# First block's output product in seven products of quarters, with the per-layer input transposed earlier and the new rows later

## The chip, the cores and the metric

The kernel runs on one core of a Trainium2 chip. The metric is the device time of one execution in microseconds (us), the median of three runs. Below, PE is TensorE (matmul), DVE is VectorE, ACT is ScalarE, POOL is GpSimd, and SP is SyncE, which here only issues transfers.

## What is computed

Two transformer blocks in a row, on 512 tokens of width 1024, in float32. The change touches the output product of the first block, the product of the per-layer input `p` that follows it, and the new rows of `x`:

```python
def first_block(x, p, w_in, b_forget, w_branch_a, w_branch_b, w_merge, w_out,
              g_pre, g_post, w_ple, w_ple_gate, g_ple):
        h = rmsnorm(x, g_pre[i])
        proj = h @ w_in[i]
...
        y_a = (att_a * jax.nn.silu(gate_a)) @ w_branch_a[i]
...
        y_b = (att_b * jax.nn.silu(gate_b)) @ w_branch_b[i]
        m_a, m_b = jnp.split(jax.nn.sigmoid(h @ w_merge[i]), 2, axis=-1)
        out = (m_a * y_a + m_b * y_b) @ w_out[i]      # 512x1024 @ 1024x1024
        x = x + rmsnorm(out, g_post[i])
        e = p[i] @ w_ple[i]                           # 512x256 @ 256x1024
        gate = jax.nn.sigmoid(x @ w_ple_gate[i])
        x = x + rmsnorm(gate * e, g_ple[i])
```

`att_b` is a forgetting attention (FOX below), `att_a` an attention over the 128 keys that an index selects (DSA below).

## The kernel before

Every float32 operand of a product is split into two parts of a shorter float format, high and low, and one product is three matmuls into the same accumulator: high by high, high by low, low by high. A matmul takes 128 rows of the contraction and 512 columns.

**Weights.** All weights are one list of groups (`stream`), in the order of use; a group of a product 512 columns wide is 256 x 512 floats (512 KB). A group is loaded from DRAM by SP into `raw` (line 308; two buffers), ACT writes its high part `wh` (line 333), DVE its low part `wl` (line 334); `wh` and `wl` have four buffers each. When a product has used up group i, `used(i)` has the groups up to three further converted and up to five further loaded. The output product has groups 54 to 61, the attentions' products, gates and branch products those before.

**The output product.** `ev_ya` makes the input of it, `m = m_a y_a + m_b y_b`, chunk by chunk (eight chunks of 128 rows by 512 tokens) and splits each into `mh` (ACT) and `ml` (DVE). `out0` and `out1` are its two halves of 512 columns: four blocks of 128 tokens by eight chunks by three matmuls each, 192 matmuls in all. `ev_out` multiplies by the gain (`ob`), takes the sum of squares on ACT, and in the second half adds to the rows `xr`; `to_T` then transposes the new rows on PE, eight transposes of a block of 128 tokens, and splits them (`x2h`, `x2l`) for the gate product `pg0`, `pg1`. Between stand `e0` and `e1`, the product of `p`, whose transposes (`pst` to `pT`) are made at the start of `out0`.

**Order.** A scheduler (the Tile framework's order of program text plus a planner) sets the order on each engine: an attention head's steps (scores S, softmax on DVE, ACT and POOL, transposes T of the probabilities, values AV) are mixed with matmuls of the products; each engine then goes through its own queue strictly in order. Transposes take turns in two PSUM banks: the next but one can only be written once the splits on ACT and DVE have read the first. In a softmax step POOL does `rr` (line 612) and the scaling of P by it (line 613).

**Sums of weights.** The last product of the kernel (down, line 1404 and on) is already made of seven products of quarters; its weight sums are built in DRAM: `plan_sums` hangs a transfer on a group's conversion. A first copy of a quarter goes by SP, without a wait. The sum is a transfer on POOL's queue that adds in DRAM; ahead of it POOL does a small copy (`poke`, line 248) that waits for that group's `wh`.

Of the kernel before, what the change touches and what calls it, by code (L numbers as in the profile page):

```python
# [11 lines left out]
F32 = mybir.dt.float32  # L12
FR = mybir.dt.float32r
# [15 lines left out]
def two_blocks_kernel(  # L29
# [11 lines left out]
    def unit(name, tag, shape=None, dt=FR):  # L41
        return pool.tile(shape or [128, 8, 512], dt, name=name, tag=tag)
# [35 lines left out]
    AHEAD = 2  # L78
    LATE = {"mla": 3, "pg1": 16, "q2": 8, "o21": 10}
    FOX = (2.0, 2, 2, 1.0)  # L80
# [28 lines left out]
    class Turned:  # L109
# [5 lines left out]
        def split(self, hi, lo, raw):  # L115
# [100 lines left out]

    def down(name):
        if name[0] == "S":  # L220
            return down_sums[name]
        f = DFF // 2 * (name[2] == "2")
        return w_down_2[f:f + DFF // 2, 512 * (name[1] == "2"):512 * (name[1] == "2") + 512]

    down_sums = {f"S{i}": tc.dram_tile([DFF // 2, 512], F32, name=f"down{i}") for i in range(1, 5)}
    DOWN = ("A11", "S4", "A12", "S1", "S2", "S3", "A22")
    specs_tail = {f"dn{name}": ([(down(name), 0, 512, 0)], 11) for name in DOWN}
    behind, poke = {}, pool.tile([128, 1], F32, name="poke", tag="poke")

    def plan_sums():  # L230

        copies = [("S1", "A21"), ("S2", "A11"), ("S4", "A12"), ("S3", "A11")]
        adds = [("S1", "A22"), ("S2", "S1"), ("S4", "S2"), ("S3", "A21")]
        for some, engine, at, step in ((copies, nc.sync, 14, 2), (adds, nc.gpsimd, first_of["seven"], 4)):
            for dst, src in some:
                for r in range(0, DFF // 2, 352):
                    behind[at] = (engine, down_sums[dst][r:r + 352, :], down(src)[r:r + 352, :])
                    at += step

# [739 lines left out]

    mh, ml = unit("mh", "U3"), unit("ml", "U6")  # L980
# [13 lines left out]

    ob = unit("ob", "U2", [128, NB, 1024], F32)
# [4 lines left out]
    x2h, x2l = unit("x2h", "U0"), unit("x2l", "U1")  # L1000

    pst = unit("pst", "U4", [128, NB, 256], F32)
    nc.sync.dma_start(pst, p.rearrange("(b p) d -> p b d", p=128))
    pT = [pool.tile([128, 2, 512], FR, name="pT", tag=f"V{i}") for i in range(2)]
    for tb in range(NB):
        to_T(pst[:, tb, :], 2, pT[0], pT[1], tb)
    gb = g_bcast(g_post)

    def ev_out(nh):
        def f(tb, ps):  # L1010
            nc.vector.tensor_mul(ob[:, tb, 512 * nh:512 * nh + 512], ps, gb[:, 512 * nh:512 * nh + 512])
            sum_sq(ps, ssq[:, tb, nh:nh + 1])
            if nh == 1:
                nc.vector.scalar_tensor_tensor(xr[:, tb, :], ob[:, tb, :], rstd2(ssq[:, tb, :], D), xr[:, tb, :],
                                               op0=OP.mult, op1=OP.add)
                to_T(xr[:, tb, :], 8, x2h, x2l, tb)
        return f
# [5 lines left out]
    eb = unit("eb", "U4", [128, NB, 1024], F32)  # L1023

# [4 lines left out]

    for nh in range(2):  # L1030
        run(product(f"e{nh}", lambda kc: (pT[0][:, kc, :], pT[1][:, kc, :]), ev_e(nh), True))

    gs = unit("gs", "U2", [128, 4, 1024], F32)
    for i, g in enumerate((g_ple, mix_norm_g_2)):
# [511 lines left out]
    def dn_banks(kinds):  # L1546
        return [{"mm": mm_bank, "S": s_bank, "AV": av_bank,
                 "T": lambda: t_bank("E").rearrange("p a b -> p (a b)")}[k]() for k in kinds]

# [23 lines left out]

    DN_ACT = {"A11": "B11", "S4": "B22", "A12": "B21", "S1": "T1", "S2": "T2", "S3": "T3", "A22": "T4"}
    DN_BANK = {"A11": ("S", "S"), "S4": ("T", "T"), "S1": ("mm", "AV"), "S3": ("T", "T"), "A22": ("S", "S")}

    def dn_product(n, name):
# [8 lines left out]
        for i, (kc, b) in enumerate(seq):  # L1586
            if n < 6 and i in (2, 8, 14):
                with tc.issue_after(mark[0]), tc.issue_after(mark_hi[0]):
                    fs_make(DN_ACT[DOWN[n + 1]], i // 6)
# [5 lines left out]
            ah, al = [t[:, kc % 4, blk(b)] for t in fs[DN_ACT[name], kc // 4]]  # L1595
# [65 lines left out]
```

## Time and profile before

| what | value |
|---|---|
| median of 3 runs | 1199.44 us (1199.09 to 1199.97) |
| the profiled execution's own time | 1198.17 us |
| span in that execution, first to last instruction | 1196.4 us |
| PE busy | 1166.9 us (98%), 6634 matmuls and transposes |
| DVE busy | 845.0 us (71%) |
| ACT busy | 637.9 us (53%) |
| POOL busy | 292.3 us (24%) |
| granted TensorE clock, mean over the span | 0.995 of full |

Times in the rows are microseconds from the start of the span. An engine's idle time is only worth something where the engine is the one that the others wait for; here PE has almost none.

### The profile page before, as it was taken

To read this page: it belongs to the slowest core of one execution; us is meant where nothing else is said; L and a number is where in the kernel's file an instruction comes from. 1 tells how busy PE (TensorE), PEld (TensorE's weight loads), DVE (VectorE), ACT (ScalarE), POOL (GpSimd) and SP (SyncE) were. 2 spreads that over 40 slices of the span, in tenths; PEclk is the share of its full clock that TensorE was granted. 3 is DMA by queue.
4 is the path that set the end of the run, shared out by engine and by line. 5 is a ranking of instruction groups with operands and counts; after the bars stand their busy time and mean duration, and the time that the engine had idled before them with its cause. 6 is when DMAs were issued, how large, how long until landed. Compare 5 with 4: busy or idle time off the path is not lost.

```text
span 1196.4 us, 18475 instructions
## 1 busy us (share of the span) xinstructions
PE 1166.9 (98%) x6634; PEld 1009.8 (84%) x6634; DVE 845.0 (71%) x1569; ACT 637.9 (53%) x1260; POOL 292.3 (24%) x500
## 2 busy tenths in 40 slices
PE   7999999999999999999999999999999999999997
PEld 5898888888888888879888878888899999998885
DVE  5578767796565753776445478874698887877895
ACT  4466356535663444544466567752555455556564
POOL 2011065403341020211333435410022212200124
PEclk9999999999999999999999999999999999999999
DMA  5423613443223523324222222155369798857553
GB/s 195 102 92 119 191 48 119 126 137 102 95 71 106 181 85 109 127 90 128 57 71 72 72 60 79 60 158 193 124 127 185 147 190 151 141 132 268 170 184 114
DMA packets 117403, 148.89 MB, mean 124 GB/s; under 512 B 15552, under 2 KB 70080, under 8 KB 117312
## 3 DMA queue, kind: packets, MB, share of 16 engines
q1 hardware_dynamic: 94528, 136.18, 36.2%
q0 software_dynamic: 22784, 11.54, 8.2%
q8 instruction: 52, 0.85, 0.3%
q14 instruction: 39, 0.32, 0.1%
HBM read 141.40 MB, written 29.36 MB: 143 GB/s over the span
## 4 chain that ended last, share of the span: by engine, by line
PE 84%; DVE 4%; issue 4%; ACT 3%; POOL 2%; DMA 2%; SPq 0%; POOLq 0%; ACTq 0%; DVEq 0%
PE mm L422 49%; PE mm L1404 7%; PE E L1404 5%; PE R L1404 5%; PE S L1597 4%; PE AV L666 3%; PE E L1597 3%; PE T L651 2%; PE mm L1597 2%; DVE wl L334 1%; ACT wh L333 1%; DMA raw<-in_w_in_dram 1%; PE T L553 1%; PE S L885 1%; PE S L884 1%
## 5 line engine op out<-in xcount | busy, mean ns | idle before, releaser
L334 DVE TENSOR_TENSOR wl<-raw,wh 128x512 fp32r<-128x512 f32 (+4 forms) x219 | 203.2, 945 | 89.3 <-ACT wh L333 88.4
L333 ACT CAST wh<-raw 128x512 fp32r<-128x512 f32 (+4 forms) x219 | 173.7, 815 | 162.2 <-PE mm L422 65.7
L612 POOL TENSOR_TENSOR rr<-rs,mone 128x1 f32<-128x1 f32 x128 | 75.5, 590 | 166.5 <-ACT P L606 106.0
L522 DVE TENSOR_TENSOR pl<-T,ph 128x128 fp32r<-128x128 f32 (+3 forms) x152 | 61.9, 412 | 60.9 <-ACT ph L521 60.2
L422 PE MATMUL mm<-hh,wh 128*128 128x512 f32 x256 | 103.5, 405 | 0.0
L422 PE MATMUL mm<-hl,wh 128*128 128x512 f32 x256 | 101.4, 396 | 0.0
L422 PE MATMUL mm<-hh,wl 128*128 128x512 f32 x256 | 100.5, 395 | 0.0
L606 ACT ACTIVATE P<-P,nm 128x128 f32<-128x128 f32 (+2 forms) x96 | 51.5, 537 | 51.4 <-DVE nm L599 47.4
L521 ACT CAST ph<-T 128x128 fp32r<-128x128 f32 (+3 forms) x152 | 54.7, 362 | 43.5 <-PE T L651 32.1
L613 POOL TENSOR_SCALAR P<-P,rr 128x256 f32<-128x256 f32 (+3 forms) x128 | 73.4, 573 | 12.0
L333 ACT CAST wh<-qsum 128x1024 fp32r<-128x1024 f32 (+1 forms) x44 | 42.8, 974 | 53.9 <-PE R L1404 16.3
L1404 PE MATMUL R<-acts,wh 128*128 128x256 f32 x320 | 57.8, 281 | 0.0
L1404 PE MATMUL mm<-acts,wh 128*128 128x256 f32 x320 | 57.6, 280 | 0.0
L651 PE MATMUL T<-ident,P 128*128 128x128 f32 x296 | 54.3, 277 | 3.3 <-ACT km L1184 2.4
L422 PEld LDWEIGHTS mm<-hh,wl 128*128 128x128 f32 x256 | 48.0, 188 | 11.2
L1404 PE MATMUL E<-acts,wh 128*128 128x256 f32 x320 | 57.1, 280 | 0.0
L334 DVE TENSOR_TENSOR wl<-qsum,wh 128x1024 fp32r<-128x1024 f32 (+1 forms) x44 | 49.3, 1122 | 11.0 <-ACT wh L333 11.0
L422 PEld LDWEIGHTS mm<-hh,wh 128*128 128x128 f32 x256 | 48.2, 188 | 8.5
L422 PEld LDWEIGHTS mm<-hl,wh 128*128 128x128 f32 x256 | 48.2, 188 | 7.8
L422 PE MATMUL mm<-h2h,wh 128*128 128x512 f32 x128 | 53.6, 419 | 0.0
L422 PE MATMUL mm<-h2h,wl 128*128 128x512 f32 x128 | 50.6, 395 | 0.0
L422 PE MATMUL mm<-h2l,wh 128*128 128x512 f32 x128 | 50.1, 392 | 0.0
(431 smaller groups left out, 3458.8 us busy)
## 6 DMA issues: line engine op xcount, KB each, us to landing
raw<-in_w_in_dram SPq DMA_DIRECT2D x50, 512.0 KB, 3.7
down<-in_w_down_dram SPq DMA_DIRECT2D x16, 704.0 KB, 6.0
quart<-in_w_up_dram SPq DMA_DIRECT2D x20, 512.0 KB, 6.4
raw<-down SPq DMA_DIRECT2D x20, 512.0 KB, 3.9
raw<-in_w_merge_dram SPq DMA_DIRECT2D x16, 512.0 KB, 4.1
raw<-in_w_out_dram SPq DMA_DIRECT2D x16, 512.0 KB, 3.9
quart<-in_w_gate_dram SPq DMA_DIRECT2D x16, 512.0 KB, 5.2
raw<-in_w_down_dram SPq DMA_DIRECT2D x15, 512.0 KB, 4.3
```

Of the source, the lines that this page charges most:

```text
L333: mark_hi[0] = nc.scalar.copy(hi[:, js], raw[:, js]).ins
L334: mark[0] = nc.vector.tensor_sub(lo[:, js], raw[:, js], hi[:, js].bitcast(F32)).ins
L422: nc.tensor.matmul(o, x_, m, start=kc == 0 and k == 0 and n0 == 0, stop=last and k == 2)
L521: nc.scalar.copy(hi, src)
L522: nc.vector.tensor_sub(lo, src, hi.bitcast(F32))
L606: nc.scalar.activation(P[:, :n], P[:, :n], AF.Exp, bias=bias, scale=-1.0, accum_out=rs)
L612: nc.gpsimd.tensor_tensor(rr, rs, mone, op=OP.pow)
L613: nc.gpsimd.tensor_scalar(P[:, :n], P[:, :n], rr, 1.0, op0=OP.mult, op1=OP.mult)
L651: nc.tensor.transpose(T[:, i, :], P[:, blk(i)], ident)
L666: nc.tensor.matmul(self.av[:, q0:q0 + pc.stop - pc.start], self.v(kb), m, start=pi == 0 and i == 0, stop=pi == len(plan) - 1 and i == 1)
L1404: nc.tensor.matmul(R[:, c, :], w[:, kc, cs], m[:, kc, :], start=first and c + kc + k == 0, stop=kc == 3 and k == 2, skip_group_check=True)
L1597: nc.tensor.matmul(acc[b], a, w[:, j], start=first and kc == 0 and k == 0, stop=kc == 10 and k == 2, skip_group_check=True)
```

## The change

The output product is done as seven products on quarters (Winograd's form of Strassen's): the tokens in two halves, the contraction in two halves, the columns in two halves. Each of the seven products is 256 tokens by 512 rows by 512 columns, that is 2 blocks of tokens x 4 chunks x 3 = 24 matmuls. The weights are the quarters A11, A12, A22 and four sums S1 to S4 of quarters, 14 groups in the place of 8; the sums are built in DRAM, by four copies of 1 MB on SP (after the conversions 14, 16, 18, 20) and four adding transfers of 1 MB on POOL (after the conversions 31, 33, 35, 37, with `poke` ahead of each). The sixteen copies for the last product follow from conversion 22 on. The inputs B11, B21, B22 are quarters of `m`, and T1 to T4 their sums: four additions on DVE, and four splits on ACT and DVE. After a product, copies, additions and subtractions in PSUM and SBUF put the four quarters of the result together (`out_end`). The order of `out`, `e0`, `e1` on PE is now that of the text (`ordered()`). The transposes of `pst` move to the start of DSA, and those of the new rows come 16 products later (`LATE`).

```diff
-    LATE = {"mla": 3, "pg1": 16, "q2": 8, "o21": 10}
+    LATE = {"mla": 3, "pg1": 16, "q2": 8, "o21": 10, "out": 16}
...
+    OUT = ("A11", "S4", "A12", "S2", "S1", "S3", "A22")
...
-        "out0": ([(w_out, 0, 512, 0)], 8),
-        "out1": ([(w_out, 512, 512, 0)], 8),
+        **quarters("out", w_out, OUT),
...
+        put(copies, nc.sync, "out", w_out, 512, [14, 16, 18, 20])
+        put([adds[i] for i in (0, 3, 1, 2)], nc.gpsimd, "out", w_out, 512, [31, 33, 35, 37])
+        put(copies, nc.sync, "dn", w_down_2, 352, list(range(22, 54, 2)))
+        put(adds, nc.gpsimd, "dn", w_down_2, 352, list(range(first_of["seven"], first_of["seven"] + 64, 4)))
...
-            elif n >= 0 and n % 5 == 2:
+            elif n >= 0 and n % 5 == 2 or 0 <= m < 14 and m % 3 == 2:
                 raw = pool.tile([128, 1024], F32, name="raw", tag="idx")
...
+    pst = q4("pst", [128, NB, 256])
+    nc.sync.dma_start(pst, p.rearrange("(b p) d -> p b d", p=128))
+    pT = [pool.tile([128, 2, 512], FR, name="pT", tag=f"V{i}") for i in range(2)]
+    for tb in range(NB):
+        to_T(pst[:, tb, :], 2, pT[0], pT[1], tb)
...
-            nc.vector.tensor_add(t, t, acc[:, i, :])
-            split(mh[:, i, :], ml[:, i, :], t, 0.5)
+            m = ta[:, i, :]
+            nc.vector.tensor_add(m, t, acc[:, i, :])
+            if g == 0:
+                split(mp["B11"][0][:, c, :], mp["B11"][1][:, c, :], m[:, 256:], 0.5)
+            else:
+                split(m21[:, 0, c, :], m21[:, 1, c, :], m, 0.5)
...
-                to_T(xr[:, tb, :], 8, x2h, x2l, tb)
+            late.append([LATE["out"], lambda: to_T(xr[:, tb, :], 8, *x2, tb)])
...
+                for k, (a, w) in enumerate(((ah, wh), (ah, wl), (al, wh))):
+                    nc.tensor.matmul(R[into][b], a, w[:, j], start=into == name and kc == 0 and k == 0,
+                                     stop=kc == 3 and k == 2, skip_group_check=True)
+                if i % 4 == 3:
+                    used(f0 + g)
...
+        T = {"T1": ("B11", "B11", OP.subtract, "B12"), "T3": ("B12", "B12", OP.subtract, "B22"),
+             "T2": ("B22", "B11", OP.add, "B22"), "T4": ("B21", "B21", OP.subtract, "B22")}
...
+        some = {(0, 4): lambda: (m_add("T1"), m_add("T3")), (1, 0): lambda: m_add("T2"),
+                (1, 4): lambda: m_part("T2", mp, 0.5), (2, 0): lambda: m_part("T1", mp, 0.5),
+                (2, 4): lambda: m_part("T3", mp, 0.5), (3, 0): lambda: m_add("T4"),
+                (3, 4): lambda: m_part("T4", mp, 0.5)}.get((n, i))
...
+            elif name == "S1":
+                c12 = p2("c12")
+                nc.vector.tensor_sub(c12, R["S4"][b], kept[b])
+                nc.vector.tensor_sub(m_sub[b], m_sub[b], R["S4"][b])
+                ev_out(0, b, c12)
...
-    run(product("out0", pair_act(mh, ml), ev_out(0), True))
-    run(product("out1", pair_act(mh, ml), ev_out(1), True, "tail"))
+    with ordered():
+        for _ in itertools.chain(
+                seven_tok("out", OUT, {"A11": ("AV", "mm"), "S4": ("S", "S"), "U": ("mm", "mm"), "A22": ("AV", "mm")},
+                          mp, out_work, out_end),
+                *[product(f"e{nh}", lambda kc: (pT[0][:, kc, :], pT[1][:, kc, :]), ev_e(nh), True)
+                  for nh in range(2)]):
+            pass
```

DVE, at the end of the branch product `ya1` and the start of the output product. In the rows, `ya<-ta,mm` takes a chunk of y_a from PSUM, the next addition makes it a chunk of m, and `ml` (before) is the low part of the chunk. Before:

```order
L986 SCALAR_TENSOR_TENSOR ya<-ta,mm 128x512 x2
L525 SCALAR_TENSOR_TENSOR ml<-ya,mh 128x512
L987 TENSOR_TENSOR ya<-ya,acc 128x512
L334 TENSOR_TENSOR wl<-raw,wh 128x1024
L987 TENSOR_TENSOR ya<-ya,acc 128x512 x2
L525 SCALAR_TENSOR_TENSOR ml<-ya,mh 128x512 x3
L522 TENSOR_TENSOR pT<-T,pT 128x2x128 x2
```

In the change, from the conversion that stands ahead of the same rows; `m_4116` is `m21`, and the addition at L1085 makes T1 first, then T3:

```order
L347 TENSOR_TENSOR wl<-raw,wh 128x1024
L1013 TENSOR_TENSOR ta<-ya,acc 128x512
L538 SCALAR_TENSOR_TENSOR m_4116<-ta,m_4116 128x512
L1011 SCALAR_TENSOR_TENSOR ya<-ta,mm 128x512 x2
L347 TENSOR_TENSOR wl<-raw,wh 128x1024
L538 SCALAR_TENSOR_TENSOR m_4116<-ta,m_4116 128x512
L1013 TENSOR_TENSOR ta<-ya,acc 128x512 x2
L347 TENSOR_TENSOR wl<-raw,wh 128x1024
L1085 TENSOR_TENSOR ta<-ta 128x4x256
L347 TENSOR_TENSOR wl<-raw,wh 128x1024
L538 SCALAR_TENSOR_TENSOR m_4116<-ta,m_4116 128x512 x2
L1085 TENSOR_TENSOR ta<-ta 128x4x256
```

The low parts of the last two chunks of m now stand behind three conversions and the addition T1; before, behind one conversion.

PE, at the start of DSA, from the third scores (384 keys) of the first head to the first transposed probabilities (`T<-ident,P`); `mm` are matmuls of a product mixed in. Before:

```order
L884 MATMUL S<-kik,qa 128x384
L885 MATMUL S<-kik,qa 128x384
L422 MATMUL mm<-hh,wh 128x512
L422 MATMUL mm<-hl,wh 128x512
L422 MATMUL mm<-hh,wl 128x512
L651 MATMUL T<-ident,P 128x128
```

In the change:

```order
L897 MATMUL S<-kik,qa 128x384
L898 MATMUL S<-kik,qa 128x384
L435 MATMUL mm<-hh,wh 128x512
L435 MATMUL mm<-hl,wh 128x512
L435 MATMUL mm<-hh,wl 128x512
L566 MATMUL T<-ident,pst 128x128 x4
L664 MATMUL T<-ident,P 128x128
```

Four of the eight transposes of `pst`, two to a bank, now stand right ahead of the first `T<-ident,P`; the other four stand, two and two, ahead of the scores of 128 and of 256 keys.

DVE beside it, from the softmax of the first scores (128 keys, `causal`) in the change; `MAX` and `MATCH_REPLACE` are the selection of the keys, `pT` the low parts of the transposed `pst`:

```order
L612 ISA P,nm<-S,causal 128x128
L347 TENSOR_TENSOR wl<-raw,wh 128x1024
L926 MAX m_2792<-mk 128x8
L889 SCALAR_TENSOR_TENSOR aa<-th,mm 128x512
L535 TENSOR_TENSOR pT<-T,pT 128x2x128
L612 ISA P,nm<-S,mk 128x256
L535 TENSOR_TENSOR pT<-T,pT 128x2x128
L927 MATCH_REPLACE mk<-m_2792,mk 128x512
L612 ISA P,nm<-S,mk 128x384
L926 MAX m_2827<-mk 128x8
L535 TENSOR_TENSOR pT<-T,pT 128x2x128 x2
```

Before, no `pT` stands here, and there is one `MAX` and one `MATCH_REPLACE` fewer between the softmax of 128 keys and the end of the selection, since that pair stood ahead of it.

POOL, at the end of FOX, in the change; `outS_81` is S1 in DRAM:

```order
L261 COPY poke<-wh 128x1
L262 DMA outS_81<-in_w_out_dram 512x4x128
L625 TENSOR_TENSOR rr<-rs,mone 128x1
L626 TENSOR_SCALAR P<-P,rr 128x256
L617 TENSOR_SCALAR bias<-nm,ctok 128x1
L625 TENSOR_TENSOR rr<-rs,mone 128x1
L626 TENSOR_SCALAR P<-P,rr 128x384
L617 TENSOR_SCALAR bias<-nm,ctok 128x1
L625 TENSOR_TENSOR rr<-rs,mone 128x1
L626 TENSOR_SCALAR P<-P,rr 128x512
```

Before, the same rows stand there without the first two. The other three pairs of `poke` and transfer (S3, then S2 from S1, then S4 from S2) stand behind the last of these rows, ahead of DSA's first `rr`.

## Rows read from the trace of the kernel before

**Rows 1.** Waits of PE over the whole run: us in total, times, longest.

```profile
PE T L553 <- DVE xn L744: 8.0, 1, 8.0
PE T L553 <- DVE xn L561: 2.7, 1, 2.7
```

**Rows 2.** Busy us by engine (PE, PEld, DVE, ACT, POOL), PEclk, DMA share, GB/s.

```profile
222.00:265.00 43.00, 43.00 (x211) 35.63 (x210) 40.09 (x99) 19.71 (x37) 6.14 (x10) 1.00 0.54 170
...
397.00:412.00 15.00, 15.00 (x71) 12.17 (x70) 11.32 (x17) 6.23 (x10) 0.00 (x0) 1.00 0.83 277
412.00:445.00 33.00, 33.00 (x147) 26.73 (x146) 14.47 (x17) 11.84 (x23) 6.49 (x10) 1.00 0.25 81
445.00:470.00 25.00, 25.00 (x121) 20.49 (x120) 10.80 (x14) 10.20 (x18) 0.93 (x2) 1.00 0.38 126
```

**Rows 3.** Chain that ended last, around the output product: start, us, what.

```profile
411.44 31.25 PE mm L422 x134
```

**Rows 4.** Timeline of DVE at the end of ya1: start, busy us.

```profile
391.60 0.68 DVE L987 TENSOR_TENSOR ya<-ya,acc 128x512 f32<-128x512 f32 x1
392.20 0.68 DVE L525 SCALAR_TENSOR_TENSOR ml<-ya,mh 128x512 fp32r<-128x512 f32 x1
...
397.01 1.21 DVE L334 TENSOR_TENSOR wl<-raw,wh 128x1024 fp32r<-128x1024 f32 x1
398.15 1.27 DVE L986 SCALAR_TENSOR_TENSOR ya<-ta,mm 128x512 f32<-128x512 f32 x2
...
402.89 1.88 DVE L525 SCALAR_TENSOR_TENSOR ml<-ya,mh 128x512 fp32r<-128x512 f32 x3
```

**Rows 5.** Timeline of ACT there.

```profile
395.27 1.06 ACT L333 CAST wh<-raw 128x1024 fp32r<-128x1024 f32 x1 [1.12 <-PE mm L422]
```

**Rows 6.** Groups of DVE by shape, whole run: busy us, mean ns.

```profile
L525 DVE SCALAR_TENSOR_TENSOR fs<-fa,fs 128x1024 fp32r<-128x1024 f32 x14 | 16.9, 1216 | 0.8 <-ACT fs L524 0.8
...
L1503 DVE TENSOR_TENSOR fa<-fa 128x1024 f32<-128x1024 f32 x8 | 10.8, 1352 | 0.0
```

**Rows 7.** Groups of DVE by shape, 375 to 470 us.

```profile
L522 DVE TENSOR_TENSOR pT<-T,pT 128x256 fp32r<-128x256 f32 x4 | 1.5, 419 | 0.8 <-ACT pT L521 0.8
```

**Rows 8.** Timeline of PE at the start of DSA.

```profile
282.58 0.33 PE L884 MATMUL S<-kik,qa 128*128 128x384 f32 x1
...
283.62 0.27 PE L651 MATMUL T<-ident,P 128*128 128x128 f32 x1
...
285.12 0.39 PE L884 MATMUL S<-kik,qa 128*128 128x512 f32 x1
```

**Rows 9.** Timeline of DVE at the start of DSA.

```profile
279.75 0.28 DVE L599 CUSTOM_DVE_ANT_0 P<-S,causal 128x128 f32<-128x128 f32 x1
...
283.63 0.55 DVE L599 CUSTOM_DVE_ANT_0 P<-S,mk 128x384 f32<-128x384 f32 x1
...
285.77 0.69 DVE L599 CUSTOM_DVE_ANT_0 P<-S,mk 128x512 f32<-128x512 f32 x1 [1.23 <-PE S L885]
```

**Rows 10.** Timeline of POOL at the end of FOX and the start of DSA.

```profile
224.73 0.92 POOL L612 TENSOR_TENSOR rr<-rs,mone 128x1 f32<-128x1 f32 x1 [0.93 <-ACT P L606]
...
229.75 0.59 POOL L613 TENSOR_SCALAR P<-P,rr 128x384 f32<-128x384 f32 x1
...
280.65 1.52 POOL L612 TENSOR_TENSOR rr<-rs,mone 128x1 f32<-128x1 f32 x1 [46.34 <-DVE m L913]
```

**Rows 11.** Chain at the end of FOX.

```profile
232.78 0.57 PE T L651 x5
```

**Rows 12.** The last product's transfers on POOL's queue, and their poke: ns min/median/max.

```profile
L249 POOL DMA_DIRECT2D down<-in_w_down_dram x8: 2126/2129/2402, 880.0 to 1043.0; - x8
...
L248 POOL COPY poke<-wh x16: 183/1238/1287, 878.9 to 1042.7; 128x1 f32<-128x1 f32 x16
```

**Rows 13.** The same transfers: KB each, median us from issue to landing.

```profile
down<-in_w_down_dram POOLq DMA_DIRECT2D x8, 704.0 KB, 10.5
down<-down POOLq DMA_DIRECT2D x8, 704.0 KB, 9.2
```

More of the change, by code (lines that the diff above doesn't have):

```diff
@@ L123, in split, with quarter, quarters @@
                                           t[..., 80 - 16 * i:96 - 16 * i].bitcast(F32))
+    in_dram = {}
+    def quarter(base, w, name):
+        n = w.shape[0] // 2
+        if name[0] == "S":
+            if (base, name) not in in_dram:
+                in_dram[base, name] = tc.dram_tile([n, 512], F32, name=f"{base}{name}")
+            return in_dram[base, name]
+        r, c = n * (name[2] == "2"), 512 * (name[1] == "2")
+        return w[r:r + n, c:c + 512]
+    def quarters(base, w, order):
+        return {base + name: ([(quarter(base, w, name), 0, 512, 0)], w.shape[0] // 256) for name in order}
+    OUT = ("A11", "S4", "A12", "S2", "S1", "S3", "A22")
     specs = {
@@ L215, in two_blocks_kernel @@
     specs["fg0"] = ([(w_gate_2, 0, 256, 0), (w_gate_2, DFF // 2, 256, 256)], 8)
[L219 to L225, printed above, removed]
     DOWN = ("A11", "S4", "A12", "S1", "S2", "S3", "A22")
-    specs_tail = {f"dn{name}": ([(down(name), 0, 512, 0)], 11) for name in DOWN}
+    specs_tail = quarters("dn", w_down_2, DOWN)
     behind, poke = {}, pool.tile([128, 1], F32, name="poke", tag="poke")
@@ L233, in plan_sums, with put @@
         adds = [("S1", "A22"), ("S2", "S1"), ("S4", "S2"), ("S3", "A21")]
-        for some, engine, at, step in ((copies, nc.sync, 14, 2), (adds, nc.gpsimd, first_of["seven"], 4)):
+        def put(some, engine, base, w, rows, at):
             for dst, src in some:
-                for r in range(0, DFF // 2, 352):
-                    behind[at] = (engine, down_sums[dst][r:r + 352, :], down(src)[r:r + 352, :])
-                    at += step
+                for r in range(0, w.shape[0] // 2, rows):
+                    behind[at.pop(0)] = [engine] + [quarter(base, w, q)[r:r + rows, :] for q in (dst, src)]
+        put(copies, nc.sync, "out", w_out, 512, [14, 16, 18, 20])
+        put([adds[i] for i in (0, 3, 1, 2)], nc.gpsimd, "out", w_out, 512, [31, 33, 35, 37])
+        put(copies, nc.sync, "dn", w_down_2, 352, list(range(22, 54, 2)))
+        put(adds, nc.gpsimd, "dn", w_down_2, 352, list(range(first_of["seven"], first_of["seven"] + 64, 4)))
     def send(i, hi):
@@ L977, in two_blocks_kernel @@
                             product("yb1", AB, ev_yb(1), False, "all")))
-    mh, ml = unit("mh", "U3"), unit("ml", "U6")
+    m21 = unit("m21", "U3", [128, 2, 4, 512])
+    m11 = unit("m11", "U6", [128, 2, 2, 4, 256])
+    mT = unit("mT", "U0", [128, 2, 2, 4, 256])
+    m4 = [pool.tile([128, 4, 256], FR, name="m4", tag=f"V{2 + k}") for k in range(2)]
+    mp = {"B11": m11[:, 0], "B22": m21[:, :, :, :256], "B21": m21[:, :, :, 256:], "T1": m11[:, 1],
+          "T2": mT[:, 0], "T3": mT[:, 1]}
+    mp = {**{n: [t[:, 0], t[:, 1]] for n, t in mp.items()}, "T4": m4}
     def ev_ya(g):
@@ new lines, in bank, with seven_tok @@
+    def bank(kind):
+        return {"mm": mm_bank, "S": s_bank, "AV": av_bank,
+                "T": lambda: t_bank("E").rearrange("p a b -> p (a b)")}[kind]()
+    ACT_OF = {"A11": "B11", "S4": "B22", "A12": "B21", "S1": "T1", "S2": "T2", "S3": "T3", "A22": "T4"}
+    def seven_tok(base, order, banks, pair, work, end):
+        R = {}
+        for n, name in enumerate(order):
+            into = {"A12": "A11", "S2": "U", "S3": "U", "S1": "S4"}.get(name, name)
+            if into not in R:
+                R[into] = [bank(k) for k in banks[into]]
+            f0 = first_of[base + name]
+            for i in range(8):
+                work(n, i)
+                kc, b = divmod(i, 2)
+                g, j = divmod(kc, 2)
+                convert_to(f0 + g)
+                wh, wl = ws[f0 + g]
+                ah, al = [t[:, kc, blk(b)] for t in pair[ACT_OF[name]]]
+                for k, (a, w) in enumerate(((ah, wh), (ah, wl), (al, wh))):
[3 more added lines that the diff above has]
+                    used(f0 + g)
+                yield 1.0
+                tick(1.0)
+            if name == "A11":
+                R["U"] = [bank(k) for k in banks["U"]]
+                for b in range(2):
+                    nc.scalar.activation(R["U"][b], R["A11"][b], AF.Copy, scale=-1.0)
+            end(name, R)
@@ new lines, in sums_of, with add, part @@
+    def sums_of(src):
+        at = {f"B{f}{t}": src[:, 4 * f - 4:4 * f, 512 - 256 * t:768 - 256 * t] for f in (1, 2) for t in (1, 2)}
+        T = {"T1": ("B11", "B11", OP.subtract, "B12"), "T3": ("B12", "B12", OP.subtract, "B22"),
+             "T2": ("B22", "B11", OP.add, "B22"), "T4": ("B21", "B21", OP.subtract, "B22")}
+        def add(name):
+            d, a, op, b = T[name]
+            nc.vector.tensor_tensor(at[d], at[a], at[b], op=op)
+        def part(name, pair, scale=None):
+            split(*pair[name], at[T[name][0]], scale)
+        return add, part
@@ L1028, in ev_e @@
         return f
-    for nh in range(2):
-        run(product(f"e{nh}", lambda kc: (pT[0][:, kc, :], pT[1][:, kc, :]), ev_e(nh), True))
-    gs = unit("gs", "U2", [128, 4, 1024], F32)
+    with ordered():
[5 more added lines that the diff above has]
+            pass
+    gs = unit("gs", "U4", [128, 4, 1024], F32)
     for i, g in enumerate((g_ple, mix_norm_g_2)):
@@ L1546, in dn_banks @@
     def dn_banks(kinds):
-        return [{"mm": mm_bank, "S": s_bank, "AV": av_bank,
-                 "T": lambda: t_bank("E").rearrange("p a b -> p (a b)")}[k]() for k in kinds]
+        return [bank(k) for k in kinds]
     def dn_end(name):
```

61 lines of the change are left out of this document (40 added, 21 removed).

## Prediction

> **What bounds the kernel now.** I read the waits of PE first. Over the whole run its longest wait is 8.0 us, at the start, and the next 2.7 us, for the rows `xn` after the gate product; none other is longer than 2.4 us [rows 1]. Then the windows: in each stretch that the change touches, PE is busy all of the time at a clock of 1.00, whatever DVE does beside it [rows 2]. The chain of waits around the output product is one long run of PE's matmuls, 134 of them in 31.25 us [rows 3], that is 0.233 us each. So PE's queue sets the time: a matmul less is worth its 0.233 us, and anything that makes PE wait is lost for good, since there is no idle time in which to make it up. Last I read DVE's and POOL's timelines at the three places where the change puts new work ahead of what PE waits for.
>
> **The change, part by part.**
>
> *Matmuls.* 192 become 7 x 24 = 168. 24 x 0.233 = **5.6 us gained**. The transposes of `pst` and of the new rows keep their number (8 and 32, some 0.11 us each [rows 11]), so moving them changes nothing on PE by itself.
>
> *First wait, the second product (S4).* It takes B22, a quarter of `m21`, in four chunks. DVE is continuously at work there. Before, the conversion that stands first in my piece of the order began at 397.01 [rows 4]. Its cover, the four low parts of `m11` ahead of it, are now 256 wide in the place of 512, some 0.26 us less each, so it begins as soon as ACT has made the high part, at 395.27 + 1.06, about 396.35 [rows 5]. From there to the third chunk's low part the order holds four conversions, eight operations 512 wide (the third chunk's own the last), and the addition T1. A conversion takes 1.14 us from one start to the next (397.01 to 398.15), a 512-wide operation 0.60 (391.60 to 392.20) [rows 4]; for the addition of 4 x 256 I take the nearest, the strided addition of 128x1024 in the last product, 1.35 [rows 6]. 396.35 + 4 x 1.14 + 8 x 0.60 + 1.35 = 407.1. The 134 matmuls of the chain's row end the output product at 411.44 + 31.25 = 442.7 [rows 3]; worked back by 192 x 0.233 and the 8 transposes of `pst`, it began at 397.0. PE wants that part in the middle of the second product, after 24 + 12 + 2 matmuls, 38 x 0.233 = 8.9 us on, at 405.9. **A wait of 1.2 us.** It would be nothing if PE came later or ACT let the conversions wait, and 2.5 us if one more conversion (1.14) had to be waited for. The fourth chunk comes 0.6 us later and is wanted 1.4 us later, so it does not wait again.
>
> *Second wait, the start of DSA.* The first `T<-P` now follows four transposes of `pst` and takes the bank that the third block of `pst` was transposed into. It was at 283.62 [rows 8]; eight transposes more, 8 x 0.11, want it at 284.5. The bank is free when DVE has made that block's low part `pT`, and in DVE's order this stands behind the softmax of 384 keys and one `MAX`. The scores of 384 keys start at 282.58 [rows 8] + 0.44 = 283.0. From a start of scores to their softmax, where DVE waited for PE, were 0.65 us (285.12 to 285.77) [rows 8, 9], so the softmax starts at 283.7; DVE itself is ready, as the softmax of 128 keys moves ahead of a `MAX` and a `MATCH_REPLACE` (about 1.2 us, to 278.55 [rows 9]), and what stands between ends by about 283.2. Then 0.55 for the softmax [rows 9], 0.60 for `MAX` (as any 512-wide operation), 0.42 for `pT` [rows 7]: 285.2. **A wait of 0.7 us**; nothing if the scheduler's neighbours come a little earlier, 1.4 if ACT's half of the split is late too. Behind it on PE stand six matmuls and the scores of 512 keys, which just move along.
>
> *POOL at the end of FOX.* The `poke` of S1 and its transfer stand ahead of `rr` at 224.73. `poke` takes 1.24 us, a transfer's issue 2.13 for 352 rows [rows 12]; for 512 rows in proportion 3.1. From about 224.1 (POOL falls idle at 224.73 - 0.93 = 223.8 [rows 10], and ACT is still making the `wh` that `poke` waits for) they hold POOL to 228.5. The scaling of P for 384 keys, at 229.75 before [rows 10], then comes at about 231.5 (`rr`, the 256-wide scaling, the bias, ACT's exponential) and ends at 232.1. PE takes it from 232.78 on [rows 11]. **Nothing**, with 0.7 us of cover; an issue twice as long would cost some 2.5 us.
>
> *The other three transfers.* S3's comes after FOX's last scaling and is waited for by nothing here. S2's waits for S1's landing: 10.5 us for 704 KB [rows 13], in proportion 15 for 1 MB, from 228.5, so 243.5. S4's waits for S2's: issued by about 247, 9.2 x 1.45 = 13.4 us [rows 13], to 260; S4's own issue is done by about 262.5. POOL has nothing else until DSA's first `rr` at 280.65, after 46.34 idle us [rows 10]. Nothing, with 18 us of cover.
>
> *The rest, at nothing.* The four copies on SP have no wait ahead of them. The weights' loads in the output product come every 2.8 us for 12 matmuls instead of every 5.6 for 24, with a third buffer; the one load that stands behind the 2 MB of `xr` in SP's queue has some 2 us before it is wanted. If it were late, each us would count. The operations that put the quarters together are read by PE through the new rows alone, whose transposes now have 16 products (3.7 us) of room.
>
> **Sum.** -5.6 + 1.2 + 0.7 = **-3.7 us**: the profiled execution took 1198.17 us, so 1194.5 is its counterpart. It lies 1.27 below the median of 1199.44, so the same forecast on the median is **1195.7 us**. 0.2%, or 2.4 us, is about what a measurement of this kernel can tell from no change.
>
> **Rivals.**
>
> *Full gain.* Both waits are hidden, since the order that I read and the moments of the chip need not meet as I laid them: 1199.44 - 5.6 = 1193.8. For it: PE had no such wait anywhere in these stretches [rows 2]. Against it: DVE is in order, and both places have its work counted out. Chance 0.12.
>
> *DVE gives most of it back.* From 397 to 470 us DVE was busy 11.32 + 14.47 + 10.80 = 36.6 us of 73 [rows 2]. The change adds 6 conversions (7.3 us at 1.21 [rows 4]), 4 additions (5.4), 4 splits of 128x1024 (4.9 [rows 6]), 8 operations on PSUM (5.4 at 0.68 [rows 4]) and takes away 4 `pT` (1.7 [rows 7]): 57.9 us of 67.4, 86%. At that share the order decides: each conversion that comes one operation too late costs some 1.2 us, and three such besides the two waits bring it to 1199.3, no change. For it: the seven products want a conversion every 2.8 us, with a chunk or sum in between. Against it: conversions run three groups, 8.4 us, ahead. Chance 0.28 for what ends within 2.4 us.
>
> *Slower: the chain of sums on POOL.* If the adding transfers S1, S2 take twice what I took from the last product (30 and 27 us), S4's issue ends at about 291, and DSA's first `rr`, in the same queue behind it, starts some 10 us late; less the 1 or 2 us that its transposes have to spare, PE loses 8 to 9, and the time is 1195.7 + 8.5 = 1204. It decides from the point where S2 lands after 278. For it: DVE is busy 40.09 of 43 us there, and reads and loads take 0.54 of the transfers' time [rows 2]. Against it: the same kind of transfer landed in 10.5 us in the last product. Beside this, the Trainium skill, page "SBUF — State Buffer", section "SBUF: two separate sides", says that a transfer issued from POOL's queue has its descriptors written by GpSimd and is starved while DVE runs operations that hold both ports; it gives 620 ns against some 3100. By that factor the chain would not land before DSA at all. The rows of the last product's transfers do not bear out such a factor. Chance 0.12, a load late behind `xr` included.
>
> **Numbers.** Forecast 0.48, full gain 0.12, DVE 0.28, slower 0.12. The forecast's own range, from the bounds of its two waits, is 1193.8 (both nothing) to 1197.7 (2.5 and 1.4), of which all but the last 0.7 is faster by over 0.2%. So faster 0.60, same 0.28, slower 0.12. For the range I go down to 1193.5 and up to 1199.8, which leaves out the slower case and a little of either end.
>
> **What would show it.** PE: 168 matmuls of the output product, the first to last some 39 us plus waits; a wait of 1.2 us of a matmul for a low part of `m21`, one of 0.7 us of `T<-P` for `pT`; nothing at the end of FOX; the first `rr` of DSA at its place; the wait of 2.7 us for `xn` unchanged. I am wrong if PE waits for `wl` or `wh` in several places of the seven products, if POOL's first `rr` of DSA waits for a transfer, or if a load of S2 is late behind `xr`.

## The result, and the profile after

The changed kernel is slower: 1207.77 us (median of 4 runs, 1206.72 to 1208.36) against 1199.70 for the kernel before beside it; the ratio is 1.0066, 95% interval 1.0054 to 1.0077. The forecast was 1195.7, the range 1193.5 to 1199.8. The profiled execution took 1207.69 us, its span is 1205.9 against 1196.4.

The page first, by engine: PE has 24 instructions fewer (6610) and is busy no shorter than before (1166.9 then).

```profile
span 1205.9 us, 18516 instructions
...
PE 1167.3 (97%) x6610; PEld 1009.3 (84%) x6610; DVE 864.2 (72%) x1591; ACT 650.3 (54%) x1278; POOL 309.3 (26%) x508
```

The waits of PE over the whole run, which answer to [rows 1]:

```profile
PE T L566 <- DVE xn L757: 8.7, 1, 8.7
PE T L566 <- DVE x2l L535: 4.0, 1, 4.0
PE T L566 <- DVE xn L574: 2.8, 1, 2.8
...
PE T L664 <- DVE pT L535: 1.4, 1, 1.4
PE S L1065 <- DVE m L538: 1.1, 1, 1.1
PE S L897 <- DVE nm L612: 0.9, 1, 0.9
...
PE mm L435 <- DVE aa L889: 0.7, 1, 0.7
```

Five of these are new: 4.0 us at the transposes of the new rows, 1.4, 0.9 and 0.7 at the start of DSA, 1.1 in the second of the seven products. That is 8.1 us, already more than the 5.6 that the 24 matmuls are worth. On PE's timeline, idle time ahead of an instruction in brackets:

```profile
281.96 0.50 PE L435 MATMUL mm<-hh,wh 128*128 128x512 f32 x1 [0.68 <-DVE aa L889]
...
285.48 0.39 PE L897 MATMUL S<-kik,qa 128*128 128x256 f32 x1 [0.92 <-DVE nm L612]
...
290.97 0.30 PE L664 MATMUL T<-ident,P 128*128 128x128 f32 x1 [1.39 <-DVE pT L535]
...
404.50 0.39 PE L1065 MATMUL AV<-wh,m 128*128 128x512 f32 x1
...
414.59 0.74 PE L1065 MATMUL S<-wh,m 128*128 128x512 f32 x2 [1.13 <-DVE m L538]
...
439.30 0.40 PE L1065 MATMUL AV<-wh,m 128*128 128x512 f32 x1
...
444.90 0.40 PE L435 MATMUL mm<-wh,pT 128*128 128x512 f32 x1
...
450.50 1.03 PE L566 MATMUL T<-ident,xr 128*128 128x128 f32 x8
455.55 1.97 PE L566 MATMUL T<-ident,xr 128*128 128x128 f32 x8 [4.01 <-DVE x2l L535]
```

The output product itself did what was forecast: from 404.50 to 444.90 are 40.40 us, less the wait of 1.13 that is 0.234 us for each of 168 matmuls. The seventh product begins at 439.30, the first transposes of new rows at 450.50, 11.2 us later: the 16 "products" of `LATE` are steps of three matmuls, 0.7 us each.

PE's clock is the rest. These windows hold the granted clock in the seventh column (after the five engines' busy times), 1.00 being 2.4 GHz:

```profile
1082.00:1094.00 12.00, 10.42 (x59) 9.26 (x58) 10.74 (x14) 8.45 (x11) 0.00 (x0) 0.86 0.69 223
450.00:460.00 10.00, 5.99 (x29) 5.06 (x28) 7.81 (x9) 4.64 (x8) 3.29 (x4) 0.83 0.66 204
240.00:265.00 25.00, 25.00 (x121) 20.56 (x121) 21.71 (x60) 8.46 (x13) 3.79 (x4) 1.00 1.25 266
190.00:202.00 12.00, 10.42 (x51) 8.40 (x49) 6.74 (x19) 6.21 (x16) 6.00 (x13) 0.86 0.52 174
```

In three of the four the clock fell to its lower level, 1.2 GHz, for a part of the window (0.14 x 12 and 0.17 x 10 are 1.7 us of lost work each). Of the kernel before, the windows 190 to 202 and 1073 to 1085 (the same place in the program as 1082 to 1094) show 1.00.

So the 9.5 us between the two spans are: -5.6 matmuls; +3.0 at DSA; +1.1 second product; +4.0 transposes; +5.1 for the three spells; +0.7 at the first wait; +0.6 for a wait at 193 us that was 0.15 before and is 0.71. That is 8.9; the other 0.6 lies in waits too small to name.

### The profile page after: what moved, and what is told of

The parts are those of the page before. It is cut to its first block, busy times and chain, and to the rows that moved or that the text cites. A ratio compares the mean times of both kernels' runs of the same rounds, so it can differ in the third digit from the quotient of the medians.

```text
span 1205.9 us, 18516 instructions
## 1 busy us (share of the span) xinstructions
PE 1167.3 (97%) x6610; PEld 1009.3 (84%) x6610; DVE 864.2 (72%) x1591; ACT 650.3 (54%) x1278; POOL 309.3 (26%) x508
## 4 chain that ended last, share of the span: by engine, by line
PE 77%; DVE 9%; issue 4%; DMA 4%; ACT 3%; POOL 3%; SPq 0%; POOLq 0%; ACTq 0%; DVEq 0%
PE mm L435 42%; PE mm L1516 6%; PE E L1516 4%; PE R L1516 4%; PE S L1707 4%; PE AV L679 3%; PE E L1707 3%; PE T L664 2%; DVE wl L347 2%; PE mm L1707 2%; DMA raw<-in_w_in_dram 2%; ACT wh L346 1%; DVE mk L927 1%; PE T L566 1%; PE S L898 1%
## 5 line engine op out<-in xcount | busy, mean ns | idle before, releaser
L347 DVE TENSOR_TENSOR wl<-raw,wh 128x512 fp32r<-128x512 f32 (+3 forms) x225 | 210.2, 951 | 83.1 <-ACT wh L346 82.4
L346 ACT CAST wh<-raw 128x512 fp32r<-128x512 f32 (+3 forms) x225 | 179.8, 821 | 158.9 <-PE mm L435 58.1
L261 POOL COPY poke<-wh 128x1 f32<-128x1 f32 x20 | 15.4, 768 | 160.5 <-ACT wh L346 160.5
```

The costliest lines, as they stand in the source:

```text
L346: mark_hi[0] = nc.scalar.copy(hi[:, js], raw[:, js]).ins
L347: mark[0] = nc.vector.tensor_sub(lo[:, js], raw[:, js], hi[:, js].bitcast(F32)).ins
```

## The experiments

Times are compared with those of the kernel before, taken beside them on the same chip; "+8.1" is the changed kernel's own distance from it. Theory: two places, the transfers of the weight sums and the order of the new rows' transposes, cost what the forecast had at nothing. The rival of each is named in its expectation.

**1. No weight sums.** S1 to S4 are not built; the products read plain quarters.

```diff
+        if base == "out" and name[0] == "S":
+            name = {"S1": "A21", "S2": "A11", "S4": "A12", "S3": "A11"}[name]
...
-        put(copies, nc.sync, "out", w_out, 512, [14, 16, 18, 20])
-        put([adds[i] for i in (0, 3, 1, 2)], nc.gpsimd, "out", w_out, 512, [31, 33, 35, 37])
```

> The four sums of the output product's weights are not built (no copies, no adding transfers, no poke); the seven products read plain quarters in their place, so the output differs. Theory: the 1 MB adding transfers at 227 to 272 us hold up the weight load issued at 232.8 (10.2 us to landing), DVE idles some 6 us, and its selection chain makes PE wait 0.7, 0.9 and part of the 1.4 us at the start of DSA. Then the load lands in about 5 us, DVE's idle time between 233 and 244 falls under 2 us, the waits of 0.7 and 0.9 are gone, the wait for pT falls to about my 0.7, and the time is about 2.3 us shorter: some 1205.5. Rival: the eight transposes of pst alone make these waits; then they stay at 3.0 us in sum and the time is the changed kernel's within 1 us.

Measured: 1204.37 against 1199.88, +4.5 (ratio 1.0041, 1.0028 to 1.0053): 3.6 us less than the changed kernel. Of the three waits at DSA one is left, 1.1 us for `pT`, 1.9 us less in sum. The profile also lost 1.7 us less to the lower clock than that of the changed kernel; whether the sums brought that on is not shown. DVE's idle time says why DSA waits less. First the changed kernel, from 225 to 246 us, the rows in which DVE sat idle:

```profile
233.33 0.29 DVE L535 TENSOR_TENSOR pl<-T,ph 128x128 fp32r<-128x128 f32 x1 [1.10 <-ACT ph L534]
...
236.24 1.29 DVE L347 TENSOR_TENSOR wl<-raw,wh 128x512 fp32r<-128x512 f32 x2 [2.01 <-ACT wh L346]
...
244.12 1.23 DVE L347 TENSOR_TENSOR wl<-raw,wh 128x1024 fp32r<-128x1024 f32 x1 [3.02 <-ACT wh L346]
```

Without the sums:

```profile
233.09 1.29 DVE L347 TENSOR_TENSOR wl<-raw,wh 128x512 fp32r<-128x512 f32 x2 [1.00 <-ACT wh L346]
240.34 1.23 DVE L347 TENSOR_TENSOR wl<-raw,wh 128x1024 fp32r<-128x1024 f32 x1 [0.33 <-ACT wh L346]
```

6.1 us idle against 1.3. Two causes come together, both in the changed kernel's rows. On POOL, S1's transfer holds the queue, so the bias of the next softmax step is late, ACT's exponential waits for it, and a weight's high part stands behind that on ACT:

```profile
226.85 3.05 POOL L262 DMA_DIRECT2D outS<-in_w_out_dram  x1
228.65 1.86 POOL L625 TENSOR_TENSOR rr<-rs,mone 128x1 f32<-128x1 f32 x1
230.62 0.47 POOL L626 TENSOR_SCALAR P<-P,rr 128x256 f32<-128x256 f32 x1
231.10 1.31 POOL L617 TENSOR_SCALAR bias<-nm,ctok 128x1 f32<-128x1 f32 x1
```

On ACT, two steps on, the exponential (`P<-P,bias`) and the high part behind it:

```profile
234.88 0.72 ACT L619 ACTIVATE P<-P,bias 128x512 f32<-128x512 f32 x1 [0.62 <-POOL bias L617]
...
235.60 1.13 ACT L346 CAST wh<-raw 128x512 fp32r<-128x512 f32 x2
```

And a weight load issued while S1 is being added took 10.2 us (median of such loads 3.7; without the sums the two loads issued there landed in 4.1). From the chain of waits, and from the list of transfers (KB, us to landing), with the two kinds of adding transfers:

```profile
232.78 10.19 DMA raw<-in_w_in_dram
```

```profile
outS<-in_w_out_dram POOLq DMA_DIRECT2D x2, 1024.0 KB, 19.1
outS<-outS POOLq DMA_DIRECT2D x2, 1024.0 KB, 19.4
```

PE did not notice at the end of FOX, as forecast. But DVE has the key selection of DSA to do there without a gap, and what it lost between 233 and 244 it still lacked at 282.

**2. The new rows apart.** The first block's transposes come 8 products after their rows instead of 16; in the changed kernel those of blocks 0 and 1 stand one behind the other.

```diff
-            late.append([LATE["out"], lambda: to_T(xr[:, tb, :], 8, *x2, tb)])
+            late.append([8 if tb == 0 else LATE["out"], lambda: to_T(xr[:, tb, :], 8, *x2, tb)])
```

> Only the first block's new rows are transposed 8 products earlier, so that the first and the second block no longer stand back to back. Theory: the 4.0 us wait arises because the second block's transposes need the two banks that DVE has not yet read (it stands behind two additions of new rows that wait for POOL); apart, the wait is under 1 us and the half clock that follows it at 455 us is gone too, 4 to 5.5 us in all: about 1203. Rival: DVE and POOL are simply late there, and the wait moves to the next transposes or to the gate product; then the time falls by less than 2 us.

Measured: 1202.54 against 1199.88, +2.7 (1.0031, 1.0020 to 1.0043): 5.4 us less. PE no longer waits there, and the clock stays at 1.00 (window 440 to 460):

```profile
444.50 1.07 PE L566 MATMUL T<-ident,xr 128*128 128x128 f32 x8
451.02 1.03 PE L566 MATMUL T<-ident,xr 128*128 128x128 f32 x8
```

```profile
440.00:460.00 20.00, 20.00 (x96) 16.27 (x95) 19.07 (x23) 14.83 (x27) 10.78 (x14) 1.00 0.53 178
```

In the changed kernel, the low parts of block 0 (`x2l`) stood on DVE behind the rows of blocks 2 and 3, and the last of these waited 0.8 us for POOL, whose square roots for four blocks took until 453.6:

```profile
451.54 1.27 DVE L1037 SCALAR_TENSOR_TENSOR xr<-ob,rstd,xr 128x1024 f32<-128x1024 f32 x1
453.61 1.28 DVE L1037 SCALAR_TENSOR_TENSOR xr<-ob,rstd,xr 128x1024 f32<-128x1024 f32 x1 [0.80 <-POOL rstd L553]
454.81 1.28 DVE L535 TENSOR_TENSOR x2l<-T,x2h 128x512 fp32r<-128x512 f32 x2
```

**3. The per-layer input back.** Its load, transposes and splits stand at the start of the output product again (the six lines from `pst = q4(...)` moved ahead of `gb = g_bcast(g_post)`).

> The load, transposes and splits of the per-layer input go back to the start of the output product; all else as changed. Theory: the wait of 1.4 us of the first transposed probabilities is gone (it is for pT), the other two waits at the start of DSA (0.7 and 0.9, from DVE's late chain) stay; at the start of the output product DVE gets 4 more operations of 0.4 us and PE's wait in the second product grows from 1.1 to some 2 us: in sum within 1 us of the changed kernel, 1207. Rival: the transposes are the whole cause at DSA; then about 3 us shorter there and 1205 to 1206 in sum.

Measured: 1208.59 against 1199.88, +8.7 (1.0078, 1.0065 to 1.0091), no gain. The profile is that of the slowest of the five executions, 1211.31 us. At the start of DSA one wait is left, 1.8 us for `aa`, where there were three of 3.0 us in sum; two new ones stand elsewhere, for `eb` at 450 us in the product of `p` and for `ph` at 355 us:

```profile
PE mm L435 <- ACT eb L1133: 2.0, 1, 2.0
PE mm L435 <- DVE aa L889: 1.8, 1, 1.8
...
PE AV L679 <- ACT ph L534: 1.3, 1, 1.3
```

So the wait for `pT` needs the transposes, and DVE's lateness remains without them: 1.8 us at 282 us, with no `pT` there. What brought the two new waits stays open. The wait in the second product stayed at 1.1 us, where both sides of the expectation had it grow.

**4. The activations' sums later.**

```diff
-        some = {(0, 4): lambda: (m_add("T1"), m_add("T3")), (1, 0): lambda: m_add("T2"),
-                (1, 4): lambda: m_part("T2", mp, 0.5), (2, 0): lambda: m_part("T1", mp, 0.5),
+        some = {(1, 4): lambda: (m_add("T1"), m_add("T3"), m_add("T2")),
+                (2, 0): lambda: (m_part("T2", mp, 0.5), m_part("T1", mp, 0.5)),
```

> The additions T1, T3 and T2 on DVE come half a product to a whole one later, behind the last low parts of m21. Theory (my first predicted wait): the addition T1 and a conversion ahead of the third chunk make PE wait 1.1 us in the second product; this wait is gone or under 0.3, nothing else moves: about 1206.7. Rival: the chain of conversions sets that wait, not the addition; then it stays over 0.8 us; or the splits of T2 and T1 come too late for their products and PE waits there instead.

Measured: 1209.98 against 1199.88, +10.1 (1.0087, 1.0073 to 1.0101). The wait of 1.1 us is gone, so the addition ahead of the third chunk made it; but the rival's second half holds, T2 is late for its own product, and a spell of the lower clock follows:

```profile
422.65 0.50 PE L1065 MATMUL mm<-wh,mT 128*128 128x512 f32 x1 [0.86 <-ACT mT L537]
424.69 1.22 PE L1065 MATMUL mm<-wh,mT 128*128 128x512 f32 x2 [1.30 <-DVE mT L538]
```

**5 to 7. The sums at other times**, each with the edit of run 2. Run 5 builds them early, run 6 spreads them over FOX, run 7 leaves them and moves the last product's copies away:

```diff
-        put(copies, nc.sync, "out", w_out, 512, [14, 16, 18, 20])
-        put([adds[i] for i in (0, 3, 1, 2)], nc.gpsimd, "out", w_out, 512, [31, 33, 35, 37])
+        put(copies, nc.sync, "out", w_out, 512, [6, 8, 10, 12])
+        put([adds[i] for i in (0, 3, 1, 2)], nc.gpsimd, "out", w_out, 512, [14, 15, 18, 21])
```

```diff
-        put([adds[i] for i in (0, 3, 1, 2)], nc.gpsimd, "out", w_out, 512, [31, 33, 35, 37])
-        put(copies, nc.sync, "dn", w_down_2, 352, list(range(22, 54, 2)))
+        put([adds[i] for i in (0, 3, 1, 2)], nc.gpsimd, "out", w_out, 512, [22, 26, 30, 34])
+        put(copies, nc.sync, "dn", w_down_2, 352, list(range(23, 31, 2)) + list(range(40, 64, 2)))
```

```diff
-        put(copies, nc.sync, "dn", w_down_2, 352, list(range(22, 54, 2)))
+        put(copies, nc.sync, "dn", w_down_2, 352, list(range(22, 30, 2)) + list(range(40, 64, 2)))
```

> The second run's edit, and the weight sums built some 100 us earlier: the copies after conversions 6, 8, 10, 12, the adding transfers after 14, 15, 18, 21, when POOL is nearly idle. Theory: the sums cost at DSA only by their traffic, as the run without sums showed (3.4 us); so the waits of 0.7 and 0.9 us at DSA are gone, the weight load of that moment lands in about 5 us, and the time is the second run's less 3: about 1199.5. Rival: the traffic costs as much wherever it stands (the stage at 75 to 130 us has weight loads too): then 1202 or more, with waits of PE for wh or wl at 75 to 150 us.

> The second run's edit, and the adding transfers spread over FOX (after conversions 22, 26, 30, 34), with POOL's softmax work around them; the last product's copies skip the conversions 31 to 39. Theory: spread, they do not hold up a weight load; the DSA waits of 0.7 and 0.9 are gone: about 1199.5, unless an issue of 3 us ahead of a softmax row of FOX makes PE wait there, 1 to 3 us (1201 to 1202). Rival: no gain, since the traffic itself is the cost.

> The second run's edit, and only the last product's copies moved away from conversions 30 to 38 (the adding transfers stay). Theory: the load that took 10.2 us was held up by the adding transfer of S1 and a copy together; without the copies in 229 to 263 us it lands in 6 to 8 us, and DVE idles some 3 us less there: 1.5 to 3 us shorter than the second run, about 1200. Rival: the adding transfers alone saturate the engines; then within 1 us of it, 1202.5.

Measured: run 5 1205.49 against 1199.99, +5.5 (1.0040, 1.0027 to 1.0052); run 6 1204.21, +4.2 (1.0031, 1.0020 to 1.0042); run 7 1200.32, +0.3 (1.0003, 0.9994 to 1.0012). Run 7 keeps its expectation in time, 2.2 us less than run 2, and the mechanism in part. The adding transfers fell from 20.1 and 18.5 us in run 2 to 14.1 and 13.2, DVE's last idle time of experiment 1 from 3.5 to 1.95, and the wait for `aa`, 1.1 us in run 2, is gone. But the load still took 9.1 us (10.6 in run 2), not 6 to 8, though without the adding transfers and with the copies (run 1) it was near 4: the adding transfer holds it up, the copies add little. The two idle times before it, behind POOL, stayed at 1.1 and 2.0 us.

Runs 5 and 6 freed DSA too, yet lost more than run 2, and miss their first expectation by 6.0 and 4.7 us. Run 5 waits 2.0 us at the start of FOX for DVE, run 6 2.0 us for block 0's new rows. Both wait longer for the last `xn` before q2, 4.4 us against 2.6 to 2.9 in runs 1 to 4 and 7. The chain of waits of run 6 there:

```profile
504.44 2.28 DVE wl L347 x2
506.74 4.73 DMA raw<-in_w_in_dram
...
515.99 1.94 PE T L566 x8
```

and of run 2:

```profile
505.63 1.15 DVE wl L347
506.79 3.61 DMA raw<-in_w_in_dram
...
515.77 1.06 PE T L566 x8
```

In runs 5 and 6 the scheduler had put two conversions in a row on DVE, and the load that waits for the second one's buffer landed later, though PE arrived some 1.6 us earlier. That the order makes the difference was not tried by itself; every run with the doubled conversion (5, 6 and 12) shows 4.4 to 4.5 us, every one without it 2.6 to 2.9.

**8. The kernel before once more.**

> The kernel before once more, for a second profile: how far the first wait (8.0 us in the profile shown, 8.7 to 9.8 in the changed kernels) and the spells of half clock (two of 3.4 us in the middle of the run, at 512 and 697 us) differ between two executions of one kernel. If the first wait again lies at 8.0 to 8.2, the changed kernels owe it to the change; if it varies by 1 us and more, it is chance.

It took 1200.35 us. The first wait was 9.2 us, so the 8.7 of the changed kernel is chance and no part of the change. So is the wait at 193 us: here 0.59, with the same 0.87 behind it as in the changed kernel, and no fall of the clock. At 1086 us the changed kernel waits

```profile
1085.00 0.50 PE L1707 MATMUL S<-wh,fs 128*128 128x512 f32 x1 [0.86 <-ACT wh L346]
1086.22 0.69 PE L1516 MATMUL mm<-t,wh 128*128 128x256 f32 x2 [0.72 <-ACT mm L1531]
```

and the kernel before the same two times, with the clock at 1.00:

```profile
1076.42 0.50 PE L1597 MATMUL S<-wh,fs 128*128 128x512 f32 x1 [0.86 <-ACT wh L333]
1077.64 0.51 PE L1404 MATMUL mm<-t,wh 128*128 128x256 f32 x2 [0.72 <-ACT mm L1419]
```

**9 to 12. Towards a version that wins.** Run 9: run 6 with all of the last product's copies after conversion 38 and the transposes 8, 20, 16 and 16 products behind their rows. Run 10: the adding transfers one conversion earlier, the copies as in run 7. Run 11: run 9 with 12 in the place of 8. Run 12: run 11's transposes without the sums (as experiment 1).

```diff
-            late.append([LATE["out"], lambda: to_T(xr[:, tb, :], 8, *x2, tb)])
+            late.append([(12, 20, 16, 16)[tb], lambda: to_T(xr[:, tb, :], 8, *x2, tb)])
```

> All together: the first block's new rows transposed 8 products earlier and the second's 4 later, the adding transfers spread over FOX (conversions 22, 26, 30, 34), the last product's copies after conversion 38. In the queues' order DVE no longer has two conversions ahead of the last rows before q2, which cost the two runs with moved sums 1.8 us of wait and a spell of half clock there. Theory: what is left against the kernel before is the gain of 5.6, the wait of 1.1 in the second product and one of about 1.2 for pT: 1200.0 - 5.6 + 2.3 = 1196.7. Rival: the issues on POOL in FOX and the denser copies beside the output product's loads cost 2 us and more: 1199 to 1201.

> As the run before it, but with the adding transfers one conversion earlier (21, 25, 29, 33), so that two of them lie ahead of FOX's first softmax rows, and with the last product's first four copies left at conversions 22 to 28, the others after 39. Theory: 1196.7 as well, within 1 us. Rival: two issues of some 4 us in a row ahead of FOX's first rows make PE wait at the start of FOX, 2 to 4 us: 1199 to 1200.5.

> As the run with all apart (1203.3), but the first block's new rows are transposed in the middle of e0 (12 products after the sixth product's end instead of 8), the second's in the middle of e1. Theory: in that run PE came to the first block's transposes 2.6 us before DVE had made the new rows, and a spell of half clock (1.7 us) followed; 4 products later (2.8 us) the wait is under 0.3 and the spell is gone: about 1199.0. Rival: DVE bounds the end of the output product, so the wait just moves to the second block's transposes or into the gate product: 1202 to 1203.

> The changed kernel with the weight sums not built (as in the first run; the output differs) and the new rows' transposes as in the run before this one: what the seven products are worth without the sums' traffic. Theory: 1207.8 - 3.4 (sums) - 5.2 (rows) = 1199.2; so the gain of 5.6 us of matmuls shows only 0.8 us, since the waits for the third chunk (1.1), for pT (1.1) and whatever PE now reaches earlier than DVE take the rest. Rival: 1196 or less, then the sums' traffic and the rows' order were all there was against the 5.6.

Measured: run 9 1203.27 against 1200.18, +3.1 (1.0025, 1.0015 to 1.0035), with a wait of 2.6 us for block 0's rows and a spell behind it; run 10 1206.36, +6.2 (1.0043, 1.0029 to 1.0058), with 1.9 us at the start of FOX and waits for POOL behind it, 3.6 us in sum where the changed kernel has 0.9; run 11 1200.48 against 1200.30, +0.2 (1.0008, 0.9997 to 1.0019); run 12 1200.44, +0.1 (1.0002, 0.9993 to 1.0011). Run 9 and run 10 miss their first expectation by 6.6 and 9.7 us, and end above the range of their rival too; run 11 is 1.5 above its own, run 12 1.2. Run 12 has neither sums nor a wait at the new rows, and still gains nothing. What it has left are 1.1 us each for the third chunk and `pT`, and at q2

```profile
512.08 1.94 PE L566 MATMUL T<-ident,xn 128*128 128x128 f32 x8 [4.48 <-DVE xn L574]
```

That last wait is 1.8 us longer than in the first profile of the kernel before (2.7). It stands behind the doubled conversion of runs 5 and 6, here without any sums, so their traffic does not make it. One more spell of the lower clock, near 1080 us, cost 1.7. With the first wait left out as chance, the profile adds up to -5.6 + 2.2 + 1.8 + 1.7 = +0.1. So run 12 does not show that the seven products are worth nothing; what they gain without the doubled conversion was not tried.

No version beat the kernel before; runs 7 and 11 equal it.

## Why the prediction was wrong

**What bounds the kernel** was right: PE's queue sets the time, and each wait on it was lost for good.

**Matmuls, -5.6:** right (0.234 us each).

**First wait, 1.2:** right, 1.13, for the third chunk's low part; experiment 4, which takes the addition T1 away from there and leaves the conversions, shows it as the cause.

**Second wait, 0.7:** the place and the bank were right, 1.39 us, inside the bounds; 1.1 when DVE is on time (run 1). The two waits ahead of it, 0.68 and 0.92 us, were not in the forecast; they belong to the next two steps.

**POOL at the end of FOX, "nothing, with 0.7 us of cover":** this step failed. The issue took 3.05 us as forecast and PE did not wait there. But I asked only who waits on PE at that moment. Delayed behind POOL were also the bias, ACT's exponential and, behind it on ACT, a weight's high part for DVE. DVE's stretch was 40.09 of 43 us busy [rows 2], and I used that row for another rival.

**The other three transfers, "nothing, with 18 us of cover":** the cover held, DSA's first `rr` did not wait for the queue. But the transfers landed in 19 us, not in the 15 and 13.4 scaled from [rows 13], and what they delayed was a load on SP's queue, which I had not asked about. Together with the step before it this is worth 3.6 us (experiment 1). Of these 1.9 us are waits at DSA, 0.3 of them part of the wait for `pT`; that the rest, which lies in the clock, is due to the sums is not shown. The slower rival had the cause in part, adding transfers slower than scaled, and the wrong way to PE. What the Trainium skill, page "SBUF — State Buffer", section "SBUF: two separate sides", says of transfers issued by POOL being starved while DVE holds the ports that the two share is not needed for the 19 us: in run 7, at the same place but freed of the copies, the same transfers landed in 14.1 and 13.2 us. No run here separates starved descriptors from shared bandwidth.

**"The operations that put the quarters together ... 3.7 us of room":** this step failed most, 4.0 us and a spell of 1.7 behind it. The 3.7 us was mis-sized: it is the time of 16 matmuls, and the steps counted are of three, so the transposes stood 11.2 us behind the sixth product. Even with three times the room PE waited: I had given the room to each block by itself, but the order had the transposes of blocks 0 and 1 back to back, 16 in a row over two banks; the second eight wait for `x2l` of the first, and that stood on DVE behind two additions, the second of which waited for POOL. Experiment 2, which only takes the two blocks apart, shows it. The bank question that I asked at DSA was the right one here too.

**The rest** is the clock: three spells in the profiled execution, one after the 4.0 us, two where waits of the same size pass without one in other executions. The granted clock of the changed kernel's four runs is 0.991 to 0.993, of the kernel before 0.993 to 0.996, so some of it is in every run. The two waits at 1086 us are the same in all fourteen profiles; the spell follows in nine of the twelve with the change and in neither of the two of the kernel before. How much of the two spells is due to the change stays open.

**The rivals:** "DVE gives most of it back" turns out right in size for the versions without the two faults: runs 7, 11 and 12 end within 0.3 us of the kernel before, with waits for `m`, `pT`, `wl` and `xn`, most of them from DVE. But its mechanism, conversions late within the seven products, was not seen: in the profile of the changed kernel the only wait there is the 1.13. That the size fits is in part luck, as run 12's sum shows.

## What to carry to other kernels

A transfer put on a queue delays more than the instruction that the critical engine takes next: follow it through each engine behind it to the one that has no gap, and ask when that engine's lateness reaches the bound, 40 us later here. Where moved steps share two banks, count the distance between neighbours, not only the distance of each from its source. A saving on an engine that is busy all the time is only a saving if the engine next to it, here DVE, arrives as early as it.

## What the runs showed of the hardware

Transfers that add in DRAM slow down under others: 1 MB landed in 18.5 to 20.1 us beside the copies (the changed kernel and run 2) and in 13 to 14 us with only the copies moved (run 7). Spreading them did not do it by itself: in run 6, with four of the copies among them, the first two still took 20.6 us. An adding transfer also holds up an ordinary load: 512 KB took 9.1 to 10.6 us beside one, 3.7 as a rule. A wait of PE can cost more than its length: after the 4.0 us the clock stood at 1.2 GHz for a while, which cost 1.7 us more. And the same two waits of 0.86 and 0.72 us were followed by such a spell in nine profiles and by none in five.
